# Three blocks of columns, not two, begun part by part in the first layer, with the shift vector multiplied on TensorE

## The chip, the cores and the metric

One core of one Trainium2 chip runs the program. The metric is device time in microseconds (us) of one execution, the median of several runs.

## The reference

Two layers over one sequence of 256 tokens with 2048 features. Each sub-layer is a residual step with a norm that a conditioning vector modulates:

```
cond = silu(c)
mod = cond @ ada_w[l] + ada_b[l]                  # [2048] @ [2048, 6 * 2048]
sh1, sc1, g1, sh2, sc2, g2 = split(mod, 6)
h = rmsnorm(x, norm_mix_g[l]) * (1 + sc1) + sh1
x = x + g1 * mixer(h)
h = rmsnorm(x, norm_ffn_g[l]) * (1 + sc2) + sh2
x = x + g2 * (silu(h @ w1) * (h @ w3)) @ w2       # d_ff 5632
```

In layer 0 the mixer projects h by w_in to four bands of 1024 columns. Bands 0 and 1 are value and gate of a causal convolution of width 31 along the tokens, with a layernorm and SiLU behind it. Bands 2 and 3 are a gated mix of tokens within chunks of 128. Both results, side by side, go through w_out. Layer 1 has a pooling mixer. A last rmsnorm ends the network. All is float32.

## The kernel before

**Products.** Tokens stand in two blocks of 128 (b = 0, 1). The transposed activations are the stationary operand, a weight streams past. Every float32 operand is cut into hi and lo, and a product is hi x hi + hi x lo + lo x hi. A *unit* (`unit`, L188) is one load of a weight of 512 x 512 (1 MB, tile `raw`), cut in two halves by ACT (`hi`, L165) and DVE (`lo`, L166), and 24 matmuls (L203, L204, L209) for both token blocks. `raw` is a ring of 5 buffers that all loads of weights and of ada_w share, `hi` and `lo` have 4 buffers each. A column block of 512 takes 4 units for the 2048 features.

**Modulation vectors.** A vector is made in pieces by generators that stand in one list (`bg`) and are taken up step by step; a step is one load of ada_w and its products. `mod_cols` (L366) makes one *part*, 512 entries of a vector, as columns: four steps, and then `put_cols` (L403). With `on_pe` the products with cond are 16 small matmuls into a PSUM bank (`ps_ada`, L379; each is two records in the trace), which ACT copies to `rows` (L396) and PE turns into columns (L408). Otherwise DVE multiplies and adds (`accq`, L384 and L388), and PE sums over the partitions (L408).

**The order of the work.** `started` (L523) begins the first layer. Its rate of background steps is 0. For each of the four parts q it finishes scale and shift of that part, scales and splits the activations (`scaled`, L494), finishes the scale of the next part, issues the units of part q of every block that is begun so, and finishes the shift of the next part. With two blocks, value columns 0 to 511 (`(w_in, 0)`) and their gates (`(w_in, DH)`), they take the four PSUM banks of `banks()`. A third block would take the two banks of the transposes (`mt`, tag "tp"); the SwiGLU of both layers uses three blocks. After part 0 the mixer's small parameters are laid out (`params`).

Behind `started` each unit ends in `after_unit`, which takes up background steps at a rate of 1.2 per unit (`RATES[0]`): first 16 steps of the gate vector g1, then 32 of scale and shift of the SwiGLU. The blocks that follow in `mixer_ab` are those at columns 512, DH + 512, the two of band 3, the two of band 2, and then `out_half(1)` and `out_half(0)` with 8 units each. `gated` (L714) multiplies value and gate, transposes, and hands the result to the convolution (`conv`, L649), whose DVE instructions (L655, L660) are put between the cuts of the weights, 5 per half unit (`FILL`). `norm_a` (L666) follows on the convolution in the same list, and `out_half(0)` needs its result. The SwiGLU of layer 0 begins with `started` again, and finishes there what steps are left of its scale and shift.

The engines take their instructions in the order that the scheduler gives them. SP issues all loads in one queue.

Of the kernel before, what the change touches and what calls it, by code (L numbers as in the profile page):

```python
# [12 lines left out]
PSUM = bass.MemoryType.PSUM  # L13
# [7 lines left out]
DH = D // 2  # L21
# [11 lines left out]
STAGED = 2  # L33
SHPE = False
# [4 lines left out]
class Trunk:  # L39
    """Activations stand in [token, feature] blocks of 128 tokens; every dense product keeps  # L40
    the transposed activations stationary and streams a weight as the moving operand.

    A float32 operand w is cut into two float32r parts, hi = round(w) and lo = w - hi, and a
    product is hi*hi + hi*lo + lo*hi, added up in float32 in PSUM."""
# [78 lines left out]
    def bands(self, tiles):  # L123
        """band[w][:, 0 and 1] takes the first 128 tokens to the trailing mean over w tokens
        minus the token, for both halves of the sequence; band[w][:, 2] the second 128 to the
        second half; band[w][:, 3] has the sums over the columns of the first, which from column
        w - 1 on are those of every later token."""
        nc = self.nc
        self.band = {}
        for w, t in zip(WINDOWS, tiles):  # L130
            nc.gpsimd.memset(t[:, :3, :], 1.0 / w)
            for n in range(w - 1):
                nc.gpsimd.memset(t[:, 0, n : n + 1], 1.0 / (n + 1))
            # token s (partition) counts for token n (free) when n - w < s <= n
            for part, off in ((0, 0), (1, P), (2, 0)):
                nc.gpsimd.affine_select(
                    out=t[:, part, :], in_=t[:, part, :], compare_op=ALU.is_ge, fill=0.0,
                    base=w - 1 - off, pattern=[[-1, P]], channel_multiplier=1,
                )
                if part != 1:  # L140
                    nc.gpsimd.affine_select(
                        out=t[:, part, :], in_=t[:, part, :], compare_op=ALU.is_ge, fill=0.0,
                        base=0, pattern=[[1, P]], channel_multiplier=-1,
                    )
                    nc.gpsimd.tensor_tensor(t[:, part, :], t[:, part, :], self.ident, op=ALU.subtract)
            self.band[w] = t
            ps = self.msp.tile([P, P], F32, name="ps_bs", tag="ms")
            nc.tensor.matmul(ps, self.ones, t[:, 0, :], start=True, stop=True)
            nc.vector.tensor_copy(t[:, 3, :], ps)

    def load_rows(self, src):
        """A vector as rows of 512 at partitions 0, 32, 64, 96, zeros elsewhere."""
# [18 lines left out]
    def filler(self):  # L171
        """One instruction of the work that runs between the cuts of the weights."""
# [15 lines left out]
    def unit(self, w, row0, col0, act, ps, first, last):  # L188
        """ps[b] += act[b] @ w[row0 : row0 + 512, col0 : col0 + 512]; act[b] = (hi, lo)."""
# [23 lines left out]
    def block(self, cells, hooks={}):  # L213
        """Units in one go, the first 128 tokens through all of them before the others.
        hooks[b, n]: what is issued ahead of half unit n of tokens b."""
# [23 lines left out]
    def tail(self, cells, resid, entry):  # L239
        """The last units of a phase: the next one's entry begins with the first 128 tokens  # L240
        while the others are still on."""
# [10 lines left out]
    def soon(self, f, *args):  # L252
        """f(*args), ahead of what else the engines could take up by then."""
        with self.tc.high_priority(SOON):
            f(*args)
# [36 lines left out]
    def mod(self, l, v, on_pe, then):  # L292
        """One modulation vector, silu(c) @ ada_w + ada_b; then(rows) gets it as four rows
        of 512, at partitions 0, 32, 64, 96."""
# [39 lines left out]
    def weighed(self, acc, l, col0):  # L334
        """acc[p, n] = the sum over k of cond[k * 128 + p] * ada_w[k * 128 + p, col0 + n]"""
# [21 lines left out]
    def mod_full(self, l, v, dst, gname=None, halves=(0, 1)):  # L357
        """A modulation vector, or half of it, as columns; see mod_cols."""
# [7 lines left out]
    def mod_cols(self, l, v, q, on_pe, dst, gname=None):  # L366
        """Part q (512 entries) of a modulation vector as columns, dst[p, k] = mod[k * 128 + p],
        or gain * (1 + mod) with a gain."""
# [54 lines left out]
    def to_bcast(self, rows, dst, n=4):  # L423
        """dst[p, :] = vector, on every partition"""
# [11 lines left out]
    def norm_cols(self, e, l, sc, sh, gname, sc_pe, sh_pe):  # L436
        """The columns of gain * (1 + scale) and of shift, in four parts each."""
# [7 lines left out]
    def bcast(self, l, v, on_pe, dst, times=None):  # L445
        """A modulation vector (times another) on every partition."""
# [9 lines left out]
    def sumsq(self, b, q):  # L456
        """The squares of a part of the residual, added up as soon as it stands."""
# [17 lines left out]
    def transposed(self, b, q, r):  # L475
        """A PSUM bank with part q of x[b] * r, transposed."""
# [17 lines left out]
    def scaled(self, src, q, b, gs, sh):  # L494
        """gs * src + sh, split: k-tiles 4q to 4q + 3 of the stationary operand."""
# [13 lines left out]
    def prep_norm(self, e, b, q):  # L509
        """act[q][b]: rmsnorm(x) * gain * (1 + scale) + shift, transposed and split."""  # L510
        e.act[q][b] = self.scaled(self.transposed(b, q, e.r[b]), q, b, e.gs, e.sh)

    def prep_late(self, e, b, q):
        """prep_norm, but for the last part, whose scale and shift come later."""
        (self.prep_norm if q < 3 else self.prep_plain)(e, b, q)

    def prep_plain(self, e, b, q):
        """The transposed x * rstd, to wait for scale and shift."""
# [4 lines left out]
    def started(self, e, w_cols, rate, then=None):  # L523
        """The first products of a layer by parts of 512 features, each as soon as its part of
        scale and shift has come."""
# [18 lines left out]
    def begun(self, e, w_cols, rest):  # L544
        """The first products of a layer, over three parts of the features and then over the
        last, as soon as its scale and shift have come."""
# [22 lines left out]
    def to_act(self, src, hi, lo):  # L569
        """src [128 tokens, 512] to split k-tiles."""  # L570
# [17 lines left out]
    def mixer_ab(self, e, nxt):  # L588
        nc, i = self.nc, self.i
        with ExitStack() as s:  # L590
# [19 lines left out]
            def params():  # L610
                """The small parameters of the mixer, laid out."""
# [21 lines left out]
            cols = [(w_in, 0), (w_in, DH), (w_in, 512)]  # L633
            held = self.started(e, cols[:STAGED], RATES[0], params)
# [31 lines left out]
            def norm_a():  # L666
                """LayerNorm over the channels, which stand on the partitions, and SiLU."""
# [45 lines left out]
            # A: gated halves, transposed to [channel, token]  # L713
# [17 lines left out]
            pv = held[2] if STAGED == 3 else proj(512)  # L731
            gated(1, pv, proj(DH + 512))
            self.late.append(lambda: self.fill.extend([conv(4), norm_a()]))

            # B: values, normed over channels, mixed over the tokens of a chunk
# [69 lines left out]
    def prep_pool(self, e, b, g):  # L805
        """The pooling runs along the tokens, so it is a product with a band over them that leaves
        the features on the partitions, where scale and shift then go in: with n = rmsnorm(x),
        band' (gs * n + sh) = gs * (band' n) + sh * (the sums over the band's columns)."""
# [129 lines left out]
    def finish_out(self, b, r):  # L938
        """The last norm; its gain is in already, but for the last part."""
# [12 lines left out]
    def run(self):  # L952
# [13 lines left out]
        self.norm_cols(mix0, 0, SC1, SH1, "mix_g", True, SHPE)  # L966
# [39 lines left out]
class Entry:  # L1006
    """What a phase needs before its first product: the norm's factor per 128 tokens, then
    parts of 512 features, prepared one by one."""
# [50 lines left out]
```

## Time and profile before

| what | us |
|---|---|
| three runs | 2018.54, 2021.42, 2023.26 |
| median | 2021.42 |
| span of the profiled execution, first to last instruction | 2018.1 |

The profiled execution has no time of its own apart from its span; the span lies 0.4 us below the fastest of the runs. In the page, PE is TensorE's matmuls, PEld its weight loads, DVE VectorE, ACT ScalarE, POOL GpSimd, SP the engine that issues the loads (SPq its queue). A timeline row has start, duration, engine, line, operation, out<-in, shape and count, and in brackets the idle time of the engine ahead of it and what ended that. Matmuls overlap: the spacing of their starts is their cost, not their duration.

### The profile page before, as it was taken

To read this page: it belongs to the slowest core of one execution; us is meant where nothing else is said; L and a number is where in the kernel's file an instruction comes from. 1 tells how busy PE (TensorE), PEld (TensorE's weight loads), DVE (VectorE), ACT (ScalarE), POOL (GpSimd) and SP (SyncE) were. 2 spreads that over 40 slices of the span, in tenths; PEclk is the share of its full clock that TensorE was granted. 3 is DMA by queue.
4 is the path that set the end of the run, shared out by engine and by line. 5 is a ranking of instruction groups with operands and counts; after the bars stand their busy time and mean duration, and the time that the engine had idled before them with its cause. 6 is when DMAs were issued, how large, how long until landed. Compare 5 with 4: busy or idle time off the path is not lost.

```text
span 2018.1 us, 23297 instructions
## 1 busy us (share of the span) xinstructions
PE 1961.8 (97%) x9039; PEld 1542.1 (76%) x9039; DVE 1384.8 (69%) x1660; ACT 837.0 (41%) x1025; POOL 36.2 (2%) x91
## 2 busy tenths in 40 slices
PE   4889999999999999999999999999999999999998
PEld 2457677668887888887878887788788888888886
DVE  3668998556777788777877788777455444554455
ACT  2333333445444343433343346544433444334443
POOL 1000000000000000000120000000000000000000
PEclk7889999999999999999999999999999999999999
DMA  9997887877888898888888886888555555555552
GB/s 327 329 380 278 318 297 285 304 283 254 286 305 316 319 330 321 306 308 313 307 322 303 301 299 232 307 319 312 187 188 187 188 188 188 187 188 190 190 188 78
DMA packets 240159, 540.30 MB, mean 268 GB/s; under 512 B 8393, under 2 KB 9721, under 8 KB 237616
## 3 DMA queue, kind: packets, MB, share of 16 engines
q1 hardware_dynamic: 238264, 536.94, 75.1%
q10 hardware_dynamic: 1784, 1.86, 0.3%
q8 instruction: 71, 1.16, 0.2%
q14 instruction: 40, 0.33, 0.0%
HBM read 536.68 MB, written 2.10 MB: 267 GB/s over the span
## 4 chain that ended last, share of the span: by engine, by line
PE 94%; DVE 2%; DMA 2%; ACT 1%; issue 0%; POOL 0%; POOLq 0%; SPq 0%; ACTq 0%; DVEq 0%
PE mm L203 28%; PE mm L204 28%; PE mm L209 27%; PE ps_ada L379 3%; PE ps_col L408 2%; PE tp L574 1%; DVE accq L388 1%; DMA x<-in_x_dram 1%; PE ps_ada L305 1%; PE mt L204 1%; PE mt L203 1%; PE mt L209 1%; PE tp L823 1%; DVE lo L166 1%; PE tp L482 0%
## 5 line engine op out<-in xcount | busy, mean ns | idle before, releaser
L166 DVE TENSOR_TENSOR lo<-raw,hi 128x1024 fp32r<-128x1024 f32 x632 | 768.4, 1223 | 435.6 <-ACT hi L165 430.7
L165 ACT CAST hi<-raw 128x1024 fp32r<-128x1024 f32 x632 | 661.1, 1053 | 930.9 <-PE mm L204 808.5
L203 PE MATMUL mm<-hi,ah 128*128 128x512 f32 x1600 | 632.3, 395 | 8.6 <-ACT hi L165 7.4
L204 PE MATMUL mm<-hi,al 128*128 128x512 f32 x1600 | 625.9, 391 | 0.0
L209 PE MATMUL mm<-lo,ah 128*128 128x512 f32 x1600 | 431.9, 390 | 2.2 <-DVE lo L166 2.2
L203 PEld LDWEIGHTS mm<-hi,ah 128*128 128x128 f32 x1600 | 301.7, 189 | 96.4 <-ACT hi L165 15.2
L209 PEld LDWEIGHTS mm<-lo,ah 128*128 128x128 f32 x1600 | 301.0, 188 | 66.2 <-DVE lo L166 3.3
L204 PEld LDWEIGHTS mm<-hi,al 128*128 128x128 f32 x1600 | 302.1, 189 | 61.9 <-issue 0.8
L203 PE MATMUL mm<-hi,hh 128*128 128x512 f32 x704 | 279.3, 397 | 0.0
L204 PE MATMUL mm<-hi,hl 128*128 128x512 f32 x704 | 277.9, 395 | 0.0
L351 DVE SCALAR_TENSOR_TENSOR acc<-raw,cond,acc 128x1024 f32<-128x1024 f32 x180 | 230.4, 1280 | 8.7 <-DMA raw<-in_ada_w_dram 7.2
L209 PE MATMUL mm<-lo,hh 128*128 128x512 f32 x704 | 194.6, 395 | 0.0
L203 PEld LDWEIGHTS mm<-hi,hh 128*128 128x128 f32 x704 | 132.1, 188 | 33.4 <-issue 0.8
L209 PEld LDWEIGHTS mm<-lo,hh 128*128 128x128 f32 x704 | 132.1, 188 | 32.2
L204 PEld LDWEIGHTS mm<-hi,hl 128*128 128x128 f32 x704 | 132.1, 188 | 31.2
L660 DVE SCALAR_TENSOR_TENSOR co<-aT,cw,co 128x256 f32<-128x256 f32 x240 | 99.1, 476 | 0.0
L582 DVE TENSOR_TENSOR gy<-mm,gate 128x512 f32<-128x512 f32 x72 | 46.9, 685 | 49.6 <-PE mm L209 49.6
L379 PE MATMUL ps_ada<-raw,cond 128*32 128x512 f32 x448 | 71.8, 677 | 5.6 <-DMA raw<-in_ada_w_dram 5.6
L203 PE MATMUL mm<-hi,mh 128*128 128x512 f32 x160 | 65.9, 413 | 0.0
L204 PE MATMUL mm<-hi,ml 128*128 128x512 f32 x160 | 63.1, 395 | 0.0
L388 DVE SCALAR_TENSOR_TENSOR accq<-raw,cond,accq 128x512 f32<-128x512 f32 x84 | 57.6, 744 | 0.0
L583 DVE TENSOR_TENSOR x<-x,gy 128x512 f32<-128x512 f32 x72 | 47.1, 686 | 0.2
(164 smaller groups left out, 939.9 us busy)
## 6 DMA issues: line engine op xcount, KB each, us to landing
raw<-in_ffn_w_dram SPq DMA_DIRECT2D x264, 1024.0 KB, 5.0
raw<-in_ada_w_dram SPq DMA_DIRECT2D x192, 1024.0 KB, 6.7
raw<-in_ab_w_in_dram SPq DMA_DIRECT2D x32, 1024.0 KB, 6.9
raw<-in_ab_w_out_dram SPq DMA_DIRECT2D x16, 1024.0 KB, 6.1
raw<-in_pool_w_dram SPq DMA_DIRECT2D x4, 1024.0 KB, 5.4
x<-in_x_dram SPq DMA_DIRECT2D x2, 1024.0 KB, 17.6
gate<-in_final_g_dram SPq DMA_DIRECT2D x1, 1024.0 KB
out_dram<-x SPq DMA_DIRECT2D x2, 512.0 KB, 3.7
```

Source lines behind the costliest of these rows:

```text
L165: nc.scalar.copy(hi, part)
L166: nc.vector.tensor_tensor(lo, part, hi.bitcast(F32), op=ALU.subtract)
L203: nc.tensor.matmul(ps[b], act[b][0][:, kk, :], hi[:, k, :], start=first and kk == 0, stop=False)
L204: nc.tensor.matmul(ps[b], act[b][1][:, kk, :], hi[:, k, :], start=False, stop=False)
L209: self.nc.tensor.matmul(ps[b], act[b][0][:, kk, :], lo[:, k, :], start=False, stop=last and kk == 3)
L351: nc.vector.scalar_tensor_tensor(acc, r2[:, j, :], self.cond[:, k : k + 1], acc, op0=ALU.mult, op1=ALU.add)
L379: nc.tensor.matmul(acc[32 * j : 32 * j + 32, :], self.cond[:, k : k + 1].to_broadcast([P, 32]), raw[:, j, :], start=u == 0, stop=u == 3, s ...
L388: nc.vector.scalar_tensor_tensor(acc[:, k % 2, :], raw[:, j, :], self.cond[:, k : k + 1], acc[:, k % 2, :], op0=ALU.mult, op1=ALU.add,)
L408: nc.tensor.matmul(ps[:, a : a + 1], src[:, P * a : P * a + P], one, start=u == 0, stop=u == len(parts) - 1,)
L582: nc.vector.tensor_tensor(t, ps, g[:, 512 * q : 512 * q + 512], op=ALU.mult)
L583: nc.vector.tensor_tensor(xs, xs, t, op=ALU.add)
L660: nc.vector.scalar_tensor_tensor(co[:, k, :], src, cw[:, k, j : j + 1], co[:, k, :], op0=ALU.mult, op1=ALU.add,)
```

## The change

Two constants and their uses go. `SHPE` becomes True: parts of the first layer's shift vector are made on PE, like those of the scale. `STAGED` becomes 3: `started` begins the value columns 512 to 1023 as well, part by part, in the banks `mt`, and the block no longer follows on its own. The rest of the diff takes comments out, so that line numbers fall by 2 to 4.

```
-STAGED = 2
-SHPE = False
...
-            cols = [(w_in, 0), (w_in, DH), (w_in, 512)]
-            held = self.started(e, cols[:STAGED], RATES[0], params)
+            held = self.started(e, [(w_in, 0), (w_in, DH), (w_in, 512)], RATES[0], params)
...
             gated(0, held[0], held[1])
             self.late.append(lambda: self.fill.append(conv(0)))
-            pv = held[2] if STAGED == 3 else proj(512)
-            gated(1, pv, proj(DH + 512))
+            gated(1, held[2], proj(DH + 512))
...
-        self.norm_cols(mix0, 0, SC1, SH1, "mix_g", True, SHPE)
+        self.norm_cols(mix0, 0, SC1, SH1, "mix_g", True, True)
```

First place, PE in the first layer, between the products of part 1 and part 2 (`mm_309` to `mm_312` are the banks of the first two blocks, `mt` those of the third, `ah` and `al` the stationary operand of a part). Before:

```order
L209 MATMUL mm_311<-lo,ah_558 128x512 x2
L209 MATMUL mm_312<-lo,ah_567 128x512 x2
L408 MATMUL ps_col<-ones,accq 128x1 x8
L379 MATMUL ps_ada<-raw,cond 32x512 x16
L408 MATMUL ps_col<-pick,rows 128x1 x4
L203 MATMUL mm_309<-hi,ah_714 128x512
```

Now:

```order
L207 MATMUL mt_313<-lo,ah_590 128x512 x2
L207 MATMUL mt_314<-lo,ah_599 128x512 x2
L377 MATMUL ps_ada<-raw,cond 32x512 x12
L406 MATMUL ps_col<-pick,rows 128x1 x4
L377 MATMUL ps_ada<-raw,cond 32x512 x16
L406 MATMUL ps_col<-pick,rows 128x1 x4
L377 MATMUL ps_ada<-raw,cond 32x512 x4
L201 MATMUL mm_309<-hi,ah_778 128x512
```

The units of a part now end with the third block, and behind them in PE's order stand three loads of the next part's shift (12 matmuls), its columns, the four loads of the scale after that, and the first load of the shift after that.

Second place, PE at the start of layer 0's SwiGLU, between its parts 2 and 3 (`mt_3349` and `mt_3350`, now `mt_3292` and `mt_3293`, are the banks of its third block). Before:

```order
L209 MATMUL mt_3349<-lo,ah_3596 128x512 x2
L209 MATMUL mt_3350<-lo,ah_3605 128x512 x2
L203 MATMUL mm_3345<-hi,ah_3721 128x512
L204 MATMUL mm_3345<-hi,al_3722 128x512
L203 MATMUL mm_3345<-hi,ah_3721 128x512
```

Now:

```order
L207 MATMUL mt_3292<-lo,ah_3539 128x512 x2
L207 MATMUL mt_3293<-lo,ah_3548 128x512 x2
L377 MATMUL ps_ada<-raw,cond 32x512 x12
L406 MATMUL ps_col<-pick,rows 128x1 x4
L201 MATMUL mm_3288<-hi,ah_3713 128x512
```

Where part 3's products followed at once, three loads of the last shift part and its columns have come in ahead of them.

Third place, DVE at the end of `norm_a`: the residuals (`gy`, `x`) of the units of `out_half(1)`, and the split (`ml`) of the convolution's result. `mm_2501` is the second of the four blocks of `out_half(1)`. Before:

```order
L698 TENSOR_TENSOR co<-co,ps_rstd 128x2048
L166 TENSOR_TENSOR lo<-raw,hi 128x1024
L414 TENSOR_TENSOR sh_140<-ps_col,adab 128x4
L582 TENSOR_TENSOR gy<-mm_2501,gate 128x512
L582 TENSOR_TENSOR gy<-mm_2502,gate 128x512
L583 TENSOR_TENSOR x_187<-x_187,gy 128x512
L492 TENSOR_TENSOR ml_2564<-co,mh_2563 128x512
```

Now, where `mm_2645` is the last of the four:

```order
L695 TENSOR_TENSOR co<-co,ps_rstd 128x2048
L164 TENSOR_TENSOR lo<-raw,hi 128x1024
L412 TENSOR_TENSOR sh_140<-ps_col,adab 128x4
L164 TENSOR_TENSOR lo<-raw,hi 128x1024
L580 TENSOR_TENSOR gy<-mm_2645,gate 128x512
L580 TENSOR_TENSOR gy<-mm_2646,gate 128x512
L581 TENSOR_TENSOR x_187<-x_187,gy 128x512
L581 TENSOR_TENSOR x_198<-x_198,gy 128x512
L490 TENSOR_TENSOR ml_2708<-co,mh_2707 128x512
```

The split of the convolution's result has moved from behind the second block of `out_half(1)` to behind the last, next to `out_half(0)`, which reads it.

## The prediction, as put on record

> **What bounds the kernel now.** I read the page first, then busy time by stretch, then the waits, then the timeline of the first 150 us.
>
> ```profile
> span 2018.1 us, 23297 instructions
> ...
> PE   4889999999999999999999999999999999999998
> ```
>
> ```profile
> 0.00:50.00 50.00, 23.11 (x97) 13.06 (x101) 16.39 (x37) 13.28 (x29) 5.38 (x18) 0.75 0.93 330
> 50.00:100.00 50.00, 42.76 (x192) 24.10 (x193) 30.46 (x53) 16.85 (x26) 0.00 (x0) 0.84 0.90 325
> 100.00:150.00 50.00, 40.41 (x198) 30.47 (x197) 34.79 (x53) 17.33 (x24) 0.00 (x0) 0.90 1.02 385
> 150.00:340.00 190.00, 190.00 (x961) 132.74 (x960) 175.64 (x333) 68.70 (x92) 2.93 (x3) 1.00 0.83 299
> ...
> 440.00:460.00 20.00, 18.24 (x111) 12.91 (x110) 14.97 (x32) 14.66 (x27) 2.00 (x2) 1.00 0.70 259
> ```
>
> Columns: stretch, length, busy time of PE, weight loads, DVE, ACT, POOL, granted clock, DMA share, GB/s. In the first 150 us PE idles 150 - 23.11 - 42.76 - 40.41 = 43.7 us at a granted clock of 0.75 to 0.90; from 150 to 340 it never idles. After 152 us the waits of PE come to 3 us in all:
>
> ```profile
> PE tp L482 <- DVE xr L479: 1.5, 2, 1.0
> PE mm L203 <- ACT ah L491: 1.2, 1, 1.2
> PE tp L823 <- DVE xc L818: 0.3, 1, 0.3
> ```
>
> So only idle PE time in the first 150 us can be won, and anything that makes PE idle later is lost whole. In the first stage the DMA queue waits for buffers of the 5-deep ring, on DVE's shift products above all (us in total, times, longest):
>
> ```profile
> SPq L182 <- DVE accq L388: 37.5, 14, 6.1
> SPq L182 <- PE ps_ada L379: 29.8, 13, 6.8
> ```
>
> **The change: prices.** PE rows:
>
> ```profile
> 46.83 3.15 PE L408 MATMUL ps_col<-ones,accq 128*128 128x1 f32 x14
> 49.91 6.56 PE L379 MATMUL ps_ada<-raw,cond 128*32 128x512 f32 x30
> ...
> 58.38 0.50 PE L203 MATMUL mm<-hi,ah 128*128 128x512 f32 x1 [0.16 <-ACT hi L165]
> ...
> 73.29 1.72 PE L408 MATMUL ps_col<-ones,accq 128*128 128x1 f32 x14 [0.22 <-DVE accq L388]
> ...
> 92.08 0.50 PE L203 MATMUL mm<-hi,ah 128*128 128x512 f32 x1
> ...
> 108.89 3.64 PE L379 MATMUL ps_ada<-raw,cond 128*32 128x512 f32 x32
> 113.24 1.05 PE L408 MATMUL ps_col<-pick,rows 128*128 128x1 f32 x8 [0.70 <-ACT rows L396]
> ...
> 118.49 0.79 PE L203 MATMUL mm<-hi,ah 128*128 128x512 f32 x1 [4.20 <-ACT hi L165]
> 119.08 0.63 PE L204 MATMUL mm<-hi,al 128*128 128x512 f32 x1
> ...
> 138.02 0.80 PE L203 MATMUL mm<-hi,ah 128*128 128x512 f32 x1 [3.06 <-ACT hi L165]
> ...
> 144.18 1.07 PE L209 MATMUL mm<-lo,ah 128*128 128x512 f32 x4
> ...
> 146.90 1.07 PE L209 MATMUL mm<-lo,ah 128*128 128x512 f32 x4
> ...
> 150.62 1.06 PE L305 MATMUL ps_ada<-raw,cond 128*32 128x512 f32 x8
> 151.61 0.50 PE L203 MATMUL mm<-hi,ah 128*128 128x512 f32 x1
> ```
>
> A half unit lasts 146.90 - 144.18 = 2.72 us, a unit 5.45. A part of scale or shift on PE (16 matmuls, 32 in the records) costs 3.64, 0.91 a load, and from its end at 112.53 the rows' copy and the columns take until 114.29, 1.76. A wait of 3.06 or 4.20 us ahead of a unit is followed by matmuls at 0.63 instead of 0.39: half rate for one or two windows, worth 1.7 to 3.4 us.
>
> Loads, and the end of the chain in this stage (SP, ACT, DVE; then the ring's landings, and DMA from 112 to 134):
>
> ```profile
> 110.02 1.23 SPq L182 DMA_DIRECT2D raw<-in_ab_w_in_dram  x2
> ```
> ```profile
> 117.39 1.99 ACT L165 CAST hi<-raw 128x1024 fp32r<-128x1024 f32 x2 [4.21 <-DMA raw<-in_ab_w_in_dram]
> ```
> ```profile
> 134.00 0.16 DVE L414 TENSOR_TENSOR sh<-ps_col,adab 128x4 f32<-128x4 f32 x1 [2.68 <-PE ps_col L408]
> ```
> ```profile
> DMA to landing us min/median/max: 5.1/7.7/10.7
> ```
> ```profile
> DMA packets 4049, 8.80 MB, mean 400 GB/s; under 512 B 137, under 2 KB 137, under 8 KB 3920
> ```
>
> With the queue full a load of 1.05 MB takes 1.05/400 GB/s = 2.6 us; alone it lands 5.1 us after its issue.
>
> **Term 1, the first stage.** PE gains 4 x 3.64 = 14.6 us of shift products, and loses 4 x about 0.9 us of columns; DVE loses 64 products. These lie in idle PE time. The third block's 4 units (21.8 us) come out of the PE-bound part. What counts is when the twelve units end. PE takes everything in order: behind the three units of a part (16.35 us) stand three loads of the next shift. In that time the ring of 5 fills with these three and two of the next scale, and DMA stops. Before, DVE took the shift's loads beside the units.
>
> - Part 0 starts at 58.38 now. 14 column products (3.15, at half clock) give way to 8, and shift loads move between the transposes; PE is slow there (30 records in 6.56 us). I take 56, between 53 (PE at full clock from 40 us on) and 60 (half clock throughout). Units 16.35 + 2.0 for the cold start: end 74.4.
> - Part 1: shift loads 3 x 0.91, tail and columns 2.1: 4.8. Then the small parameters as now, from 75.01 (73.29 + 1.72) to 92.08, 17.1, plus one shift load 0.9, less some 2 us of half clock that PE, busy until then, should escape: start 74.4 + 20.8 = 95.2, end 111.6.
> - Part 2: the first shift load is done 0.95 later, that frees a buffer, 5.1 until its load lands, three more at 2.6 (the last is the first weight), 0.6 for a late landing, 1.05 for its cast: 15.5. Start 127.1, units 16.35 + 2.0 cold: end 145.4.
> - Part 3: shift loads 2.73 and tail 0.35, columns 1.76, and 3.4 to the first product (now 138.02 - 134.00 = 4.0; one cast moves ahead of another) with hand-overs: 8.4. Start 153.8, end 153.8 + 16.35 + 1.7 = 171.9.
>
> Now the second block ends and the next starts at 151.61; with 21.8 us for the third block less 1.2 for matters that merely move, the equal point is 172.2. Term 1 is -0.3, with bounds -4 and +4: nearly the whole of the third block is paid back as ring stalls and cold starts.
>
> [...]
>
> **Term 2, cover of the convolution.** DVE's 248 convolution instructions start after the first block has been gated, and norm_a must end before out_half(0). Four units fewer stand between. The rows are the stretches of the convolution and of what follows, DVE's split of the result (third order excerpt), and the first matmul of out_half(0):
>
> ```profile
> 160.50:336.40 175.90, 175.90 (x892) 121.79 (x891) 167.40 (x327) 62.30 (x84) 2.93 (x3) 1.00 0.84 301
> ```
> ```profile
> 364.08 2.49 DVE L492 TENSOR_TENSOR ml<-co,mh 128x512 fp32r<-128x512 f32 x4
> ```
> ```profile
> 392.05 0.50 PE L203 MATMUL mm<-hi,mh 128*128 128x512 f32 x1
> ```
>
> Convolution ends 184.8 us after 151.61, its result for the first 128 tokens at 364.08 + 0.7, 28.4 us later; PE needs it 55.7 us after the convolution. Now that cover shrinks by the 21.8 us and by some 3.4 us of scale products and columns that move behind, to 30.5; DVE has two sets of residuals more in the same stretch (8 x 0.6 = 4.8), 172 of 176 us. Cover 25.7 to 30.5 against 28.4: I take 1.0, bounds 0 and 4. It is hidden today by 27 us.
>
> **Term 3, start of the first SwiGLU.** The rate of background steps is 1.2 per unit; 4 units fewer leave 5 of the 48 steps undone, and they come up where the rate is 0: a scale load and four shift loads. Three of these and the columns stand bare between part 2 and part 3 (the second order excerpt). Their PE work is not new; the wait is: copy of the rows 0.7, then from the shift columns to the first product 2.0 and 0.4 to its second operand, 3.1 in all, no other product being ready. Nearest row: 3.06 before 138.02, which also cost half rate. I add 1.1 for that (two chances in three of 1.7): 4.2, bounds 2.5 and 6. Before, this place costs 20.00 - 18.24 = 1.8, which stays.
>
> [...]
>
> **Sum.** -0.3 + 1.0 + 4.2 = +4.9 us on the 2018.1 us of the span: 2023.0. The runs shown are 2018.54, 2021.42 and 2023.26; the profiled span sits with the lowest, so against the median 2021.42 the forecast is 2026.3.
>
> **Rivals.**
> - *Faster: DMA alone sets the stage.* If PE's order did not hold the ring, the stage would grow by four loads: 4 x 2.6 = 10.4, the twelve units would end at 150.7 + 10.4 = 161 instead of 172, and 11 would be won, less the 5.2 of the two later terms: -6, 2015.5. For it: 43.7 us of idle PE, and 37.5 us of DMA queue waits on DVE that vanish. Against: shift loads stand behind 16.35 us of units in PE's order. It decides if the ring frees a buffer within 5 us of filling. 0.18.
> - *No change: half of it.* The stage ends about 167 and wins 5, and the two later waits take 5 back: 2021. For it: the bounds of part 0 and of the cold starts. 0.32.
> - *Forecast: slower by 2.5 to 8.* 0.38.
> - *Slower by more: DVE becomes the bound.* 172 of 176 us leaves little. Were DVE late by its added 4.8 us and the norm's chain bare with 28.4 against 20, some 8 us would be idle at out_half(0): +12, 2033. Against: in this trace DVE at 167.40 of 175.90 never makes PE wait. 0.12.
>
> A measurement of this kernel tells about 0.2% (4 us) from no change. The forecast and the last rival give slower 0.50, no change 0.32, faster 0.18. The range reaches from near the faster rival's time, 2016, to the last one's, 2033; what lies below and above holds some 2 in 10.
>
> **What the new profile would show.** Right: idle PE in the first 170 us near 40 us still; the third block's products (mt) ending near 172; waits of PE for hi after DMA ahead of parts 2 and 3; SP waiting on ps_ada, no longer on accq; PE idle for 3 us at the start of the first SwiGLU (near 460) behind ps_col. Wrong: mt's last product ahead of 166, or no wait at the SwiGLU's start (then no change or faster); waits of PE on lo, ps_ln or ml between 180 and 400 beyond 4 us (then the DVE rival).

## The result, and the profile after

| | before | after |
|---|---|---|
| runs, us | 2018.26, 2018.54, 2021.42, 2023.26 | 2028.71, 2028.90, 2029.14, 2033.28 |
| median, us | 2019.98 | 2029.02 |
| ratio of the runs | 1 | 1.0052, interval 1.0040 to 1.0064 |
| span of the profiled execution, us | 2018.1 | 2027.4 |

The change makes the kernel 0.52% slower, about 10 us; the two profiled spans lie 9.3 us apart. One run of a kernel below ("third block, first stage uncut"), 2824.65 us at a mean granted clock of 0.649, is left out of its ratio. First the busy times of the changed kernel by the stretches of before (columns as there):

```profile
0.00:50.00 50.00, 25.73 (x147) 9.92 (x147) 9.22 (x28) 16.47 (x36) 4.96 (x18) 0.83 0.89 328
50.00:100.00 50.00, 45.98 (x227) 28.31 (x224) 19.76 (x28) 18.89 (x25) 0.00 (x0) 0.93 0.95 356
100.00:150.00 50.00, 44.84 (x235) 29.07 (x233) 11.54 (x21) 12.24 (x19) 0.00 (x0) 0.90 0.81 305
...
440.00:460.00 20.00, 17.63 (x95) 12.13 (x94) 15.50 (x31) 16.04 (x29) 1.46 (x1) 0.91 0.70 263
```

In the first 150 us PE is busy for 116.6 us instead of 106.3: the shift products and a third block are in there. From 440 to 460, where before it worked 18.24 us at full clock, it now works 17.63 us at 0.91.

The waits of the DMA queue in the first 170 us, the two longest groups (total, times, longest):

```profile
SPq L180 <- PE ps_ada L377: 70.6, 27, 10.0
SPq L180 <- DVE lo L164: 28.7, 10, 4.9
```

The 37.5 us on DVE's `accq` are gone, but the 29.8 us on `ps_ada` have become 70.6, with single waits of 10.0 us. Busy times in a stretch in which the units of part 0 run, before the change:

```profile
60.00:80.00 20.00, 16.70 (x79) 12.09 (x78) 16.66 (x27) 4.78 (x8) 0.00 (x0) 0.84 1.05 404
```

and in the changed kernel:

```profile
60.00:80.00 20.00, 19.30 (x106) 13.24 (x104) 4.60 (x9) 4.13 (x8) 0.00 (x0) 1.00 0.80 301
```

The DMA share, the last column but one, was 1.05; now it is 0.80. While PE is in the units of a part, the queue stands still for a time.

The first products of parts 0 and 1 in the timeline of PE:

```profile
55.60 0.79 PE L201 MATMUL mm<-hi,ah 128*128 128x512 f32 x1 [1.15 <-ACT hi L163]
...
92.92 0.50 PE L201 MATMUL mm<-hi,ah 128*128 128x512 f32 x1
```

and those of parts 2 and 3, with a scale load ahead of part 2 that DMA brings late:

```profile
118.20 1.06 PE L377 MATMUL ps_ada<-raw,cond 128*32 128x512 f32 x8 [1.48 <-DMA raw<-in_ada_w_dram]
...
124.40 0.79 PE L201 MATMUL mm<-hi,ah 128*128 128x512 f32 x1 [0.71 <-ACT hi L163]
...
151.54 0.79 PE L201 MATMUL mm<-hi,ah 128*128 128x512 f32 x1 [2.40 <-ACT hi L163]
```

Third block's last products (tile `mt`; the last start is the second number behind the median):

```profile
L207 PE MATMUL mt<-lo,ah x32: 388/389/389, 69.7 to 170.5; 128*128 128x512 f32 x32
```

The products of `mt` end about 171. Behind that, the waits of PE to the end of the program:

```profile
PE mm L201 <- ACT ah L489: 4.0, 2, 2.1
PE tp L480 <- DVE xr L477: 1.9, 3, 1.0
PE ps_col L406 <- ACT rows L394: 0.7, 1, 0.7
...
PE mm L202 <- DVE ml L490: 0.2, 1, 0.2
```

And the two places of the first SwiGLU at which they lie, its entry

```profile
453.98 0.91 PE L201 MATMUL mm<-hi,ah 128*128 128x512 f32 x2 [1.97 <-ACT ah L489]
454.69 0.63 PE L202 MATMUL mm<-hi,al 128*128 128x512 f32 x1
```

and the place between its parts 2 and 3:

```profile
505.26 2.78 PE L377 MATMUL ps_ada<-raw,cond 128*32 128x512 f32 x24
508.75 1.05 PE L406 MATMUL ps_col<-pick,rows 128*128 128x1 f32 x8 [0.71 <-ACT rows L394]
511.86 0.79 PE L201 MATMUL mm<-hi,ah 128*128 128x512 f32 x2 [2.06 <-ACT ah L489]
...
513.18 0.63 PE L201 MATMUL mm<-hi,ah 128*128 128x512 f32 x1
```

Both waits are followed by matmuls at 0.63 instead of 0.39, half the clock. Before, the first of them was 1.2 us long with no slow clock behind it, and the second was not there.

**Where the 9.3 us come from.** All kernels here have the same 7584 matmuls of products (512 columns, with `hi` or `lo`) on PE. The start of the k-th of them in two traces, subtracted, says what was won or lost up to that point. Four marks are used: the 289th (twelve units done), the 1153rd (start of the first SwiGLU), the 1393rd (10 of its units done) and the last. A kernel that has done fewer background steps at a mark has to make up for them: 0.91 us a step, 1.8 for two parts' columns, 1.1 for the transposes of `gated`, which three blocks bring behind the mark. At the four marks the changed kernel stands at -7.2, -5.6, +9.2 and +9.3. At the first it owes 4 steps and the transposes (4.7), at the second 5 steps and two columns (6.4). So it has gained 2.5 in the first stage, lost 3.2 between the first stage and the first SwiGLU, and lost 8.5 at the start of that.

### The profile page after: what moved, and what is told of

Same layout as the page of the kernel before. It is cut to its first block, busy times and chain, and to the rows that moved or that the text cites. A ratio compares the mean times of both kernels' runs of the same rounds, so it can differ in the third digit from the quotient of the medians.

```text
span 2027.4 us, 23426 instructions
## 1 busy us (share of the span) xinstructions
PE 1975.8 (97%) x9135; PEld 1541.3 (76%) x9135; DVE 1346.2 (66%) x1596; ACT 839.7 (41%) x1029; POOL 36.1 (2%) x91
## 4 chain that ended last, share of the span: by engine, by line
PE 77%; ACT 0%; DVE 0%; issue 0%; POOL 0%; POOLq 0%; DVEq 0%
PE mm L201 24%; PE mm L202 23%; PE mm L207 23%; PE tp L572 1%; PE ps_col L406 1%; PE ps_ada L377 1%; PE mt L207 1%; PE mt L202 1%; PE mt L201 1%; PE tp L819 1%; PE ps_ada L319 0%; PE tp L480 0%; PE ps_bc L430 0%; PE ps_bc L431 0%; DVE lo L164 0%; ACT hi L163 0%
## 5 line engine op out<-in xcount | busy, mean ns | idle before, releaser
L201 PE MATMUL mm<-hi,ah 128*128 128x512 f32 x1568 | 621.1, 396 | 8.3 <-ACT hi L163 4.2
L202 PE MATMUL mm<-hi,al 128*128 128x512 f32 x1568 | 615.5, 393 | 0.0
L207 PE MATMUL mm<-lo,ah 128*128 128x512 f32 x1568 | 424.1, 391 | 0.0
L201 PEld LDWEIGHTS mm<-hi,ah 128*128 128x128 f32 x1568 | 297.0, 190 | 98.0 <-ACT hi L163 17.8
L202 PEld LDWEIGHTS mm<-hi,al 128*128 128x128 f32 x1568 | 297.3, 190 | 62.0 <-issue 0.8
L207 PEld LDWEIGHTS mm<-lo,ah 128*128 128x128 f32 x1568 | 295.9, 189 | 62.1
L377 PE MATMUL ps_ada<-raw,cond 128*32 128x512 f32 x576 | 90.0, 648 | 6.9 <-DMA raw<-in_ada_w_dram 6.9
L207 PE MATMUL mm<-lo,mh 128*128 128x512 f32 x160 | 46.3, 397 | 0.0
## 6 DMA issues: line engine op xcount, KB each, us to landing
x<-in_x_dram SPq DMA_DIRECT2D x2, 1024.0 KB, 17.3
```

The costliest lines, as they stand in the source:

```text
L201: nc.tensor.matmul(ps[b], act[b][0][:, kk, :], hi[:, k, :], start=first and kk == 0, stop=False)
L202: nc.tensor.matmul(ps[b], act[b][1][:, kk, :], hi[:, k, :], start=False, stop=False)
L207: self.nc.tensor.matmul(ps[b], act[b][0][:, kk, :], lo[:, k, :], start=False, stop=last and kk == 3)
L377: nc.tensor.matmul(acc[32 * j : 32 * j + 32, :], self.cond[:, k : k + 1].to_broadcast([P, 32]), raw[:, j, :], start=u == 0, stop=u == 3, s ...
```

## The experiments

The same reckoning for every kernel, each profiled once and timed in five rounds beside the kernel before (in the reckoning, minus is won; "cut steps" are explained with the third group):

| kernel | ratio to before | first stage | between | first SwiGLU | rest | cut steps between |
|---|---|---|---|---|---|---|
| before | 1 | 0 | 0 | 0 | 0 | 1 |
| the changed kernel | 1.0052 | -2.5 | +3.2 | +8.5 | +0.1 | 5 |
| shift on PE only | 1.0006 (0.9993 to 1.0019) | -1.3 | 0 | 0 | -1.3 | 1 |
| third block only | 0.9996 (0.9987 to 1.0005) | -9.7 | +1.4 | +6.0 | +0.2 | 2 |
| rate 1.4 | 1.0053 (1.0038 to 1.0069) | -3.6 | +17.3 | -2.5 | -1.5 | 9 |
| shift ahead of third unit | 1.0038 (1.0023 to 1.0053) | -0.8 | +6.3 | +2.1 | -1.4 | 5 |
| third block, SwiGLU order | 0.9961 (0.9948 to 0.9973) | -10.5 | +1.3 | +1.5 | -1.3 | 2 |
| changed, SwiGLU order | 1.0015 (1.0005 to 1.0024) | -1.8 | +4.8 | +2.1 | -1.3 | 5 |
| changed, steps uncut | 1.0060 (1.0048 to 1.0073) | -2.4 | +7.8 | +6.0 | -1.1 | 0 |
| changed, shift between units | 1.0017 (1.0008 to 1.0026) | -7.6 | +4.8 | +8.6 | -1.3 | 5 |
| left over only | 1.0049 (1.0035 to 1.0062) | +2.1 | +1.7 | +7.0 | 0 | 2 |
| changed, both orders | 1.0000 (0.9991 to 1.0009) | -6.4 | +5.2 | +3.8 | -1.4 | 5 |
| third block, first stage uncut | 1.0004 (0.9994 to 1.0015) | -3.0 | +2.1 | +3.8 | -1.4 | 4 |
| before, steps cut on purpose | 1.0200 (1.0186 to 1.0215) | +4.6 | +35.4 | +0.3 | -1.4 | 31 |

Two things limit how far one profile can be read. Kernels whose first stage has the same instructions in the same order on PE, DVE and ACT still differ there: the kernel before and "left over only" by 2.1 us, the changed kernel, "rate 1.4" and "changed, SwiGLU order" by up to 1.8. So a difference of 2 us in that column is not read.

The other is the granted clock. It falls to half for one or more stretches of 3.41 us (what stood ahead of it in two kernels is in the last section). Where PE never idles, as from 349.40 to 352.81 in the kernel before, such a stretch costs 1.6 us: eight products start 0.43 us apart instead of 0.23. The -1.3 in the rest is one such stretch, from 1257.34 to 1260.76 in the kernel before and from 1266.75 to 1270.16 in the changed one. A wait of PE in layer 1 stands ahead of it, 1.00 us in the one and 1.01 in the other; only the four kernels with about 0 in that column have the stretch. Between the first stage and the first SwiGLU the kernel before has one, in `norm_a` from 349.40 to 352.81, and so have most others. The changed kernel and "third block, first stage uncut" have none; "rate 1.4" and "shift ahead of third unit" have two in `norm_a`. So at an equal clock the changed kernel loses not 3.2 but 4.8 us between. At the start of the first SwiGLU the changed kernel has two, from 454.37 and from 512.40 on, "third block only" and "left over only" one each.

### Each half of the change alone

In the kernel before:

```
-SHPE = False
+SHPE = True
```

> Two blocks begun part by part as before, the shift vector of the first layer on TensorE as in the changed kernel. Theory (the changed kernel loses its time by the start of the first SwiGLU, where 5 steps are left over): 40 units stand behind the two blocks, so no step is left over, the start of the first SwiGLU looks as before with a wait of 1.2 us and no slow clock, and the shift products fit into idle TensorE time; total within -5 and +1 us of the kernel before. Rival (the 128 additional shift matmul records, 14.6 us less 4.2 us of columns, are added to a TensorE that is the bound): +8 to +11 us, wherever they stand.

Measured: 1.0006, no change. With two blocks the 14.6 us of shift products cost nothing: the first stage is as long as before, within what a profile can tell. The rival of work that is simply added is out.

```
-STAGED = 2
+STAGED = 3
```

> Three blocks begun part by part, the shift vector still multiplied on DVE. Theory: 36 units stand behind, 5 steps are left over, and the start of the first SwiGLU costs the same 8 to 9 us over the work that moves there as in the changed kernel; the first stage may gain up to 5 us; total +3 to +9 us against before. Rival (shift products on TensorE are the loss): TensorE has none of their 10.4 us, so at most +1 us.

Measured: 0.9996, below what the theory expected. The number is the rival's, but the kernel just shown has the same shift products on TensorE and loses nothing by them. The start of the first SwiGLU costs its 6.0, but the first stage wins 9.7 us and not "up to 5". The products of `mt` end near 164, 7 us ahead of the changed kernel:

```profile
L209 PE MATMUL mt<-lo,ah x32: 389/389/389, 71.7 to 163.3; 128*128 128x512 f32 x32
```

and the DMA share is 1.03 in a stretch (columns as above)

```profile
100.00:125.00 25.00, 20.21 (x110) 14.88 (x110) 17.62 (x30) 7.36 (x11) 0.00 (x0) 0.87 1.03 382
```

in which the changed kernel has 0.80:

```profile
100.00:125.00 25.00, 21.40 (x125) 12.43 (x124) 3.70 (x11) 5.65 (x10) 0.00 (x0) 0.90 0.80 300
```

So neither half is the loss. Together they are: the shift on PE takes 7.2 of the 9.7 us that the third block brings, and only in its company.

### What holds the first stage

> The changed kernel, but in the first stage the next part's shift loads and columns stand ahead of the third block's unit in TensorE's order instead of behind it, rate 1.2 as there. Theory (TensorE's order holds the five buffers, so the DMA queue stands still in the units): buffers come free after 10.9 us of units instead of 16.35, the columns' latency lies beside the third unit, and the third block's last product comes 5 to 10 us before 171 us; the loss at the first SwiGLU stays; total 4 to 9 us below the changed kernel. Rival (loads alone set the stage): last product at 171 within 2 us, total unchanged.

```
             for u, (w, col0) in enumerate(w_cols):
+                if u == 2 and q < 3:
+                    self.finish(e.parts[q + 1])
                 self.unit(w, 512 * q, col0, e.act[q], ps[u], q == 0, q == 3)
```

Measured in the first stage: no gain, `mt` ends near 173 against the 5 to 10 us ahead of 171 that were expected. For this stage that is what the rival said; the next kernel, with the same loads, tells the two apart. The 1.0038 comes from the first SwiGLU, where the same lines mend the order (below), which was not foreseen either. The timeline shows why the first stage stays:

```profile
115.36 0.79 PE L201 MATMUL mt<-hi,ah 128*128 128x512 f32 x1 [3.06 <-ACT hi L163]
```

PE now waits 3.06 us for the first weight of the third block's unit, and again at 148.10, 6.1 us in the two waits. Three loads, their columns and a fourth load in one piece on PE hold the ring in either place: up to 175 us the queue waits 72.5 us on `ps_ada`, 9.8 at the longest. The wait has only been moved.

The next kernel gives the matmuls of the first stage's background steps a scheduling priority, so that the loads of the shift come one by one between the units (`atom` is 500 from ahead of `started` to behind it and 1 elsewhere; the four matmuls in `mod` get the same line):

```
-                    nc.tensor.matmul(
-                        acc[32 * j : 32 * j + 32, :], self.cond[:, k : k + 1].to_broadcast([P, 32]), raw[:, j, :],
-                        start=u == 0, stop=u == 3, skip_group_check=True,
-                    )
+                    with self.tc.high_priority(self.atom):
+                        nc.tensor.matmul(
+                            acc[32 * j : 32 * j + 32, :], self.cond[:, k : k + 1].to_broadcast([P, 32]), raw[:, j, :],
+                            start=u == 0, stop=u == 3, skip_group_check=True,
+                        )
```

> The changed kernel, with that priority for the steps of the first stage alone: the next part's shift loads come between the units of a part in TensorE's order, one by one, instead of behind them. Theory (in TensorE's order the shift loads behind 16 us of units hold the buffers of the ring, which DVE's products did not): the third block's last product comes near 164 us as with the shift on DVE, not 171; 5 to 8 us faster than the changed kernel. Rival (14.6 us of shift products and 5 us of slow clock set the stage, wherever they stand): last product at 170 or later, within 2 us of the changed kernel.

Measured: `mt` ends near 166, the first stage is 5.1 us shorter than in the changed kernel, and the whole 0.35% faster than it. The products are the same, and so is DVE's part; what is new is their place on PE. The DMA queue's waits on the steps:

```profile
SPq L181 <- PE ps_ada L380: 50.9, 23, 3.0
```

and the products of `mt`:

```profile
L208 PE MATMUL mt<-lo,ah x32: 388/389/498, 72.4 to 165.5; 128*128 128x512 f32 x32
```

The waits on `ps_ada` fall from 70.6 to 50.9 us and the longest from 10.0 to 3.0. Those on `lo` rise from 28.7 to 37.6, but the DMA share from 100 to 125 us is 0.99 instead of 0.80. With the loads one by one 5.1 of the 7.2 us come back; about 2 stay open.

### The start of the first SwiGLU

In the changed kernel, more steps per unit behind the first stage, so that none is left over:

```
-RATES = 1.2, 0.71, 0.5, 1.0, 1.0
+RATES = 1.4, 0.71, 0.5, 1.0, 1.0
```

> The changed kernel with 1.4 background steps per unit instead of 1.2 behind the first stage, so that 36 units take up all 48 steps. Theory: nothing is left over, the waits of 0.7 and 2.1 us between parts 2 and 3 of the first SwiGLU and the two stretches of half clock near 455 and 513 us go, 6 to 8.5 us against the changed kernel; the time is within 3 us of the kernel before. Rival (work of TensorE, not its place, sets the time): within 2 us of the changed kernel. Second rival (DVE and DMA have no room for more steps beside the convolution): waits on lo or raw appear between 180 and 400 us and eat at least half of the gain.

Measured: 1.0053, as the changed kernel. The loss at the first SwiGLU is gone, as the theory had it, and it comes back in full between the first stage and there. The first rival's number came true, but not its reason: the 17.3 us come on top of the steps' own work, which the reckoning has taken out. It is not the second rival either, since PE hardly waits:

```profile
PE tp L480 <- ACT ah L489: 2.1, 1, 2.1
PE mm L201 <- ACT hi L163: 0.9, 2, 0.7
PE mm L207 <- DVE lo L164: 0.7, 2, 0.5
```

The wait of 2.1 us, for `ah`, is the one at the entry of the SwiGLU, which here stands ahead of the mark instead of behind it. Most of the 17.3 us is PE's own time; the group on cut steps says whose. In the kernel before, the opposite, a rate at which the 40 units leave 5 steps over:

```
-RATES = 1.2, 0.71, 0.5, 1.0, 1.0
+RATES = 1.08, 0.71, 0.5, 1.0, 1.0
```

> The kernel before, with 1.08 background steps per unit instead of 1.2, so that its 40 units leave 5 of the 48 steps over as in the changed kernel, and nothing else of the change. Theory (the left-over steps cost 6 to 8.5 us beside their own work): +5 to +9 us against before, with the wait of 2.1 us behind the shift columns and the half clock behind it at the start of the first SwiGLU. Rival (steps that move cost nothing, the loss there comes with the third block): within 2 us of before.

Measured: 1.0049, at the upper end of what was expected and as slow as the changed kernel, with nothing else of it. The rows are those of the changed kernel:

```profile
506.96 2.78 PE L379 MATMUL ps_ada<-raw,cond 128*32 128x512 f32 x24
510.45 1.05 PE L408 MATMUL ps_col<-pick,rows 128*128 128x1 f32 x8 [0.71 <-ACT rows L396]
513.56 1.22 PE L203 MATMUL mm<-hi,ah 128*128 128x512 f32 x2 [2.06 <-ACT ah L491]
```

Of its 10.7 us in the profile 7.0 lie at the first SwiGLU, 1.7 between (one cut step more, below), and 2.1 in a first stage that the edit doesn't touch. So the left-over steps alone cost 7 us beside their own work, in this one profile. Last, the lines of `started` shown above, for the SwiGLU alone (`if u == 2 and q < 3 and then is None`), once in the changed kernel and once in the kernel with the third block only:

> The changed kernel with only that order at the start of the first SwiGLU; the first stage is the changed kernel's. Theory: 5 to 6.5 us faster than the changed kernel, +3 to +5 us against before. Rival (work, not place): within 1 us of the changed kernel.

> The third block with the shift vector on DVE, and at the start of the first SwiGLU the left-over shift loads stand ahead of the third block's unit instead of behind it. Theory (third block alone wins 9 us in the first stage and loses 6 of the moved steps' bare waits and slow clock at the first SwiGLU): the wait of 2.1 us and the half clock near 505 us go, 3 to 5 us against the kernel with the third block alone; 4 to 7 us faster than before. Rival (what is lost there is TensorE work that must stand somewhere): as the kernel with the third block alone, within 1 us of it.

Measured: 1.0015, and 0.9961. The timeline of the second:

```profile
487.73 2.78 PE L379 MATMUL ps_ada<-raw,cond 128*32 128x512 f32 x24
490.44 0.50 PE L203 MATMUL mt<-hi,ah 128*128 128x512 f32 x1
...
491.47 0.95 PE L408 MATMUL ps_col<-pick,rows 128*128 128x1 f32 x8
492.28 0.48 PE L203 MATMUL mt<-hi,ah 128*128 128x512 f32 x1
```

The same three loads and columns stand there, with products between and behind them, no wait and no slow clock. Both gain at least what was expected (5.5 us in the spans for the first; 6.9 for the second, where 3 to 5 were expected), though 1.4 and 1.5 of it lie in the rest. The kernel with the third block, the shift on DVE and this order is 0.39% faster than before and the fastest of all: it beats both.

With both orders in the changed kernel:

> The changed kernel with both orders: in the first stage the shift loads between the units, and at the first SwiGLU the left-over shift loads ahead of the third block's unit. Theory (two separate losses): the gains of 4.8 and 5.5 us of the two kernels alone add up to 10 us against the changed kernel, -3 to +1 us against before. Rival (a shorter first stage only moves the wait to another place, the convolution or the first SwiGLU): 5 to 7 us against the changed kernel.

Measured: 1.0000. Against the changed kernel that is 0.52%, the 10 us of the theory (8.1 in the profiled spans). The change as it was meant, with its order mended twice, is no faster than before.

### Steps that are cut

A background step is four matmuls (8 records) on four groups of 32 columns. In the kernel before, a whole one, and one whose first matmul is parted from the other three by the transposes of `gated`:

```profile
197.85 1.06 PE L305 MATMUL ps_ada<-raw,cond 128*32 128x512 f32 x8
198.85 0.50 PE L203 MATMUL mm<-hi,ah 128*128 128x512 f32 x1
...
211.61 1.04 PE L305 MATMUL ps_ada<-raw,cond 128*32 128x512 f32 x2
212.59 0.66 PE L724 MATMUL tp<-ident,at 128*128 128x128 f32 x4
213.18 1.06 PE L305 MATMUL ps_ada<-raw,cond 128*32 128x512 f32 x6
214.17 0.50 PE L203 MATMUL mm<-hi,ah 128*128 128x512 f32 x1
```

The whole step holds PE from 197.85 to 198.85, 1.00 us. The first matmul alone holds it from 211.61 to 212.59, 0.98, and the other three from 213.18 to 214.17, 0.99. So a cut step costs 0.98 us more. Between the first stage and the first SwiGLU, before has 1 of these, the changed kernel 5, the kernel with rate 1.4 has 9.

> The changed kernel, with a scheduling priority for the four matmuls of a background step between the first stage and the first SwiGLU, so that no other instruction comes between them. In the changed kernel 5 steps are cut there in 2 + 6 records, in the kernel before 1, and a cut step takes two times 0.98 us instead of one. Theory: 4 to 5 cuts fewer are worth 3 to 5 us against the changed kernel. Rival (the additional 0.98 us lies beside other work or only moves): within 1 us.

The edit is the priority shown above, set behind `started` instead. Measured: 1.0060, no gain. The cuts are gone, and the matmuls of the steps hold PE for about 4 us less, but waits have come in their place (total, times, longest):

```profile
PE tp L483 <- DVE xr L480: 2.3, 3, 1.5
PE mm L202 <- ACT mh L492: 1.5, 1, 1.5
PE tp L759 <- DVE vv L752: 1.0, 1, 1.0
```

Nothing follows from it on the price, since the priority moves other work too. In the kernel with the third block and the order mended, the same priority in the first stage:

> The third block with the shift vector on DVE and the order of the first SwiGLU mended, and in the first stage the four matmuls of a scale step kept together, 3 of which are cut at 79 to 89 us at 0.98 us each. Theory of the cut's price: 2 to 3 us faster than without. Rival (the loads set this stage now: the DMA share there is 0.98 to 1.03): within 1 us of the kernel without.

Measured: 1.0004 against 0.9961 without: neither the theory nor the rival. In the profile the first stage is 7.5 us longer, and the granted clock shows where (last column but two). Without the priority:

```profile
70.00:90.00 20.00, 18.53 (x95) 9.47 (x93) 10.54 (x21) 5.15 (x11) 0.00 (x0) 1.00 1.02 386
```

and with it:

```profile
70.00:90.00 20.00, 17.03 (x80) 9.32 (x79) 7.89 (x17) 3.37 (x7) 0.00 (x0) 0.69 0.88 321
```

The clock is 0.69 where it was 1.00, and 0.71 in the 20 us behind. The first row at the lower clock is at 77.74 (four transposes of the parameters in 1.09 us, where the other kernel has 0.65), ahead of the place of the first step that is cut in the other kernel (79.93), so it isn't the cuts that are gone which bring it down. Products are at 0.63 up to 100.87 and at 0.39 from 101.63 on. What does bring the clock down is not shown. Apart from the one left out, the runs of this kernel lie between 2014.22 and 2022.92 us, at mean granted clocks of 0.987 to 0.980, so the profile shows one of several outcomes, and the price can't be read from it. The price itself is settled by a kernel that cuts on purpose, in the kernel before, between the first stage and the first SwiGLU:

```
                 for j in range(4):
+                    with self.tc.high_priority(self.cut if j == 0 else 1):
```

> The kernel before, with the first of the four matmuls of some 30 background steps between the first stage and the first SwiGLU moved one to four matmuls ahead of the other three, and nothing else of the change. Theory (a cut step takes two times 0.98 us of TensorE instead of one, and nothing hides that where TensorE never idles): 25 to 32 us slower than before. Rival (the second 0.98 us lies beside the product between the two pieces): within 3 us of before.

Measured: 1.0200, 39 us more span with 30 cuts more. The new pattern:

```profile
204.59 1.04 PE L307 MATMUL ps_ada<-raw,cond 128*32 128x512 f32 x2
205.56 0.50 PE L210 MATMUL mm<-lo,ah 128*128 128x512 f32 x1
205.99 1.06 PE L307 MATMUL ps_ada<-raw,cond 128*32 128x512 f32 x6
206.98 0.50 PE L204 MATMUL mm<-hi,ah 128*128 128x512 f32 x1
```

35.4 us lie between the first stage and the first SwiGLU, 1.18 a cut: 0.98 of the step, 0.2 of the products around it. By this price the 4 cuts more of the changed kernel are 4.7 us, and at an equal clock it loses 4.8. The other kernels with 4 cuts more, counted with one stretch of half clock as in the kernel before, lose 4.7 to 5.2; the one with 3 more loses 3.7 (3.5 by the price), and those with one more lose 1.3 to 1.7 (1.2). Of the 17.3 us of rate 1.4, 8 cuts are 9.4, 2.5 only moved from behind the mark, one stretch of half clock more is 1.6, and waits other than at the entry are 1.6; about 2 stay open.

## Why the prediction was right or wrong, point by point

**The sign and the size.** Slower was forecast, by 4.9 us on the span, and it is 9.3 (10 by the ratio). The sum is half of what was measured, and the measured loss lies above the 2.5 to 8 that the forecast had its chance of 0.38 for, short of the last rival. Term 3, whose mechanism held, gives the sign, but has half its size; the cut steps are not in the sum; and term 1 was too high by 2.2, which hides part of what was missing.

**Term 1, the first stage: -0.3, measured -2.5 (bounds -4 to 4).** The parts were forecast to start at 56, 95.2, 127.1, 153.8 and to end at 171.9; they start at 55.6, 92.9, 124.4, 151.5 and end near 171. The same first stage is at -3.6 and -1.8 in two other profiles, all within the bounds. The reason given, that PE's order holds the ring and stops DMA, holds: loads between the units give 5.1 us back. Half of what was off is the end, 171.9 against 170.75 for the start of the 289th product. The other half is the equal point: 172.2 was forecast, and the 289th product of before, at 178.0, less the 4.7 us of work done ahead, makes it 173.3. The 1.2 us taken off "for matters that merely move" were a mistake. Of the signs, PE's idle time in the first 170 us is 35.0 us, not "near 40". Missing in the working: the price of the ring is not in the third block, but in both edits at once. With DVE on the shift the third block alone ends near 164, close to the 161 of the rival in which DMA alone sets the stage.

**Term 2, the cover of the convolution: +1.0, measured 0.2.** The cover did shrink: DVE's split of the result (`ml`) is at 388.06 now, not 364.08, and PE starts on it at 388.8 with a wait of 0.2 us, where 27 us had been to spare:

```profile
388.06 2.50 DVE L490 TENSOR_TENSOR ml<-co,mh 128x512 fp32r<-128x512 f32 x4
```

So the term was sized about right, where the estimate could have gone to 4. But this stretch loses 3.2 us all the same, 4.8 at an equal clock, and the step that failed is the premise that "only idle PE time in the first 150 us can be won" and only a wait can be lost later: the change shifts background steps against other work of PE, so that 5 are cut instead of 1, and PE is slower there without idling. That stood in the order of the instructions and was not priced.

**Term 3, the first SwiGLU: +4.2 (2.5 to 6), measured 8.5.** 5 steps were left over as counted, and the bare wait stood between parts 2 and 3 as said, though at 508 to 512, not "near 460". It costs 0.71 + 2.06 of wait and 1.9 of slow clock, and with the hand-overs 5.0 us at this place; 4.2 was near. The step that failed is that the 1.8 us of before at the entry were taken as what "stays": near 454 the wait of 1.19 us grew to 1.97, the clock dropped there too (1.6 us), and the transposes got a second wait of 0.4. In all that is 3.0 us more; the last 0.5 goes with the two loads and columns that stand between products near 487. In the kernel with left-over steps alone that entry has the wait of 1.97 too, without the slow clock, so that part of the loss doesn't come with the wait alone (last section).

**The rivals.** DVE as the bound: no, PE waits for `lo` nowhere behind 160 us. DMA alone: not in this kernel, but in the half of the change without shift on PE. No change: the first stage won 2.5 and not 5, and what followed took 11.7 and not 5.

**The clock.** The prediction gave half rate behind the wait between parts 2 and 3 two chances in three, after the row of 3.06 us ahead of 138.02. The trace shows half the clock behind 2.06 us: from 508.99 to 512.40 us PE is busy for 1.35 of 3.41 us at a clock of 1.00, and from 512.40 to 515.81 the clock is 0.50. The 1.1 us that the prediction added for this were right in kind; 1.9 were measured. Why the clock fell there is not shown.

## What to carry to other kernels

A piece of work that moves from one engine into another engine's idle time need not be free there. Here it stood behind the units in PE's order and held the buffers of the loads until its turn: the longest wait of the DMA queue on `ps_ada` was 10.0 us, and the DMA share beside the units was 0.80, where it had been 1.05. Behind two units of 5.45 us the move cost nothing here, behind three 7.2 us. When a stage is made longer in units and the units pace a background list, count what is left of the list where the pace ends, and place it ahead of work that is ready rather than behind the last of it. Each half of a change is worth a run: here one half with one change of order is 0.39% faster, and both halves are 0.52% slower.

## What the runs showed of the hardware

- In the kernel before, four matmuls with 32 columns each, into four groups of 32 partitions, hold PE for 1.00 us together (197.85 to 198.85), and one of them alone for 0.98 (211.61 to 212.59). Parted by one or two other matmuls, in the kernel with steps cut on purpose, the four cost 1.18 us more (35.4 us for 30). Why is not shown.
- The granted clock of TensorE is 1.0 or 0.5 in all records of the traces of the kernel before and of the changed kernel. Each record but the last lasts 3.41 us or a whole multiple of it; those at half last 3.41 to 20.48 us in the first 160 us, and 3.41 each behind that. Five are behind that, and this is what PE did in the 3.41 us ahead of each fall:

| kernel | 3.41 us ahead of the fall | PE busy, us | wait of PE in it, us |
|---|---|---|---|
| before | 345.99 to 349.40 | 3.41 | none |
| before | 1253.93 to 1257.34 | 2.41 | 1.00 |
| changed | 450.96 to 454.37 | 1.44 | 1.97 |
| changed | 508.99 to 512.40 | 1.35 | 2.06 |
| changed | 1263.34 to 1266.75 | 2.40 | 1.01 |

The first, in `norm_a`, has no wait: products with one column (`ps_var`) are 2.38 us of it, PE never idles, and the clock falls all the same.

```profile
345.99:349.40 3.41, 3.41 (x26) 3.21 (x27) 0.83 (x3) 0.00 (x0) 0.33 (x1) 1.00 0.63 238
349.40:352.81 3.41, 3.41 (x9) 2.65 (x9) 2.24 (x3) 1.04 (x1) 1.28 (x1) 0.50 0.40 109
```

- A wait of the same length did not cost the same in two kernels. At the entry of the first SwiGLU the changed kernel waits 1.97 us, and half the clock follows:

```profile
450.96:454.37 3.41, 1.44 (x10) 1.08 (x11) 2.32 (x6) 3.38 (x9) 0.00 (x0) 1.00 1.05 408
454.37:457.78 3.41, 3.41 (x10) 2.67 (x9) 2.09 (x6) 2.10 (x4) 0.00 (x0) 0.50 1.05 410
```

In the kernel with left-over steps alone the same wait is 1.97 us too, and the products behind it take 0.40, not 0.63:

```profile
457.24 0.74 PE L203 MATMUL mm<-hi,ah 128*128 128x512 f32 x2 [1.97 <-ACT ah L491]
457.82 0.40 PE L204 MATMUL mm<-hi,al 128*128 128x512 f32 x1
```

What tells the two apart is not shown, and no kernel was built to try it.
